# Hybrid attention and delta-rule layer on one core: the planner's date for the first products of the triangular inverse moves from 0.3 to 1.5

## The chip, the cores and the metric

The kernel runs on one core of a Trainium2 chip. The metric is device time in microseconds (us) of one execution, as the median of a few executions. A trace of one execution gives busy times of the engines: PE is TensorE (matmuls; PEld is its weight loads), DVE is VectorE, ACT is ScalarE, POOL is GpSimd, and SP is SyncE, which here only issues transfers.

## What is computed

One layer over 512 tokens of width 1024: a norm, one wide input projection, an attention branch, a delta-rule branch (8 heads, forward and backward, in chunks of 64 tokens), gates, output projections and two more norms. The part that the change touches is the inverse of a unit triangular matrix in each chunk of the delta rule:

```python
decay = jnp.exp(jnp.where(tril, g[..., :, None] - g[..., None, :], -jnp.inf))
L = jnp.tril(jnp.einsum('bhncd,bhnjd->bhncj', k_beta, k) * decay, -1)
T = lax.linalg.triangular_solve(eye + L, jnp.broadcast_to(eye, L.shape),
                                left_side=True, lower=True, unit_diagonal=True)
u = jnp.einsum('bhncj,bhnjv->bhncv', T, v_beta)
w = jnp.einsum('bhncj,bhnjd->bhncd', T, k_beta * jnp.exp(g)[..., None])
```

Behind it a scan over the chunks carries a state per head and direction; its output is normed, gated and projected together with the attention branch.

## The kernel before

**Matrix products in three passes.** A float32 weight slab of 128x1024 is loaded (`wraw`), ACT rounds it to `whi` (a CAST), and DVE or POOL subtracts to get the rest, `wlo`. A product is then lo·hi + hi·lo + hi·hi over 8 pieces of the contraction: lines 534, 535 and 536 in `gemm_t` (a "gemm step" below is one such group of three matmuls of 128x512), and 553 to 555 or 571 to 573 in `gemm_n` and `gemm_k`. This is most of TensorE's work, and it does not depend on the delta rule: slab follows slab in the order that the string `ORDER` gives.

**The delta rule beside it.** The 8 heads go in two groups, g = 0 and g = 1, each with two directions d. For each group `phase_a` makes the triangular blocks (lines 1013 and 1018 on PE, products on DVE), inverts the 32x32 diagonal blocks by 30 dependent steps on DVE (lines 1049 and 1051, tiles `blk`), sends the result through DRAM (`dW`) and gets it back in two tiles `c2`. From these, four copies on ACT write the diagonals of `LT[0]`, four transposes on DVE write `VT[0]`, four copies on ACT write `VT[1]` (the tile of the name `blk` in the trace, line 1084), and four transposes on DVE write the diagonals of `LT[1]`. Then PE merges 32-blocks into 64-blocks, in 64 products at line 1094 (`m1`) and, after a copy of `m1` to SBUF by ACT (line 1100, a tile `c2`), 64 products at line 1107 (`v1`); each is recorded as two small matmuls, so 128 in the trace. Lines 1127 and 1142 merge 64-blocks into 128-blocks in the same way. `phase_b` then scans the chunks: lines 1177 and 1188 multiply with the state, DVE subtracts (line 1181), line 1197 applies the inverse, line 1215 makes the state's increment, line 1221 updates the state on DVE, line 1229 makes the output.

**What sets the order.** Each engine runs its own list of instructions in the order in which they were issued, and that order is fixed when the program is built. A planner, the class `Flow`, decides it with a clock of its own. Every part (a gemm stream, a phase, the tail of a slab) is a generator. `yield "at", t` asks to go on when the planner's clock has reached t, `yield "get", tag` asks for a free buffer, `yield "pe", d` says that PE is taken for d us. Of the parts that are ready, the one with the smallest priority number goes first, so `phase_a` (priority 1) goes before the gemm stream (priority 10) as soon as its date is reached; until then the gemm stream fills PE, if its next slab is due in the planner's clock. Work on the other engines is booked into the first gap of that engine's plan that is long enough, with a fixed estimate of its duration:

```python
def slot(self, engs, dur, dep):
    t = max(self.now + 0.2, dep + 0.15)
    while True:
        at = [self.fit(e, dur, t) for e in engs]
        if all(a == t for a, _ in at):
            return t, [i for _, i in at]
        t = max(a for a, _ in at)
```

So a date in one part moves not only that part. All that is booked after it sees another clock, another set of gaps and other free buffers. `either` (line 237) takes whichever of two engines would finish first in the plan, so an operation can change its engine as well. The dates decide only the order; on the chip an instruction waits for its inputs by semaphores, whatever the plan thought.

The wait at line 1087 stands behind the copies and transposes of lines 1076 to 1085, whose planned ends are `t0`, `t1` and `ready`, and ahead of the products of line 1094.

Of the kernel before, what the change touches and what calls it, by code (L numbers as in the profile page):

```python
# [35 lines left out]
class Flow:  # L36
# [70 lines left out]
    def free(self, tag, t=None):  # L107
        self.slots[tag].append(self.now if t is None else t)
# [75 lines left out]
def layer(ctx, tc, x, xT, pw0, wp1, wt, wba, wn, rows, qkn, hd16, npost, pnorm, dnorm, cs, out):  # L184
# [12 lines left out]
    def A(dur, dep, fn, *a, **k):  # L197
        return op("ACT", dur, dep, fn, *a, **k)

    def V(dur, dep, fn, *a, **k):  # L200
        return op("DVE", dur, dep, fn, *a, **k)
# [793 lines left out]
    def phase_a(g):  # L995
# [11 lines left out]
        ready = 0.0  # L1007
        for c in range(NT):
# [16 lines left out]
            ready = max(ready, tm)  # L1025
# [50 lines left out]
        for q in range(4):  # L1076
            r, lc = r32(q), r32(q % 2)
            t0 = A(0.53, tx[0], act.copy, LT[0][r, :, r], cx[0][r])
            t1 = V(0.6, max(tx[0], tv[0]), dve.transpose, VT[0][r, :, lc], cx[0][r])
        ready = max(t0, t1)  # L1080
        free("c2", ready)
        for q in range(4):
            r, lc = r32(q), r32(q % 2)
            t0 = A(0.53, max(tx[1], tv[1]), act.copy, VT[1][r, :, lc], cx[1][r])
            t1 = V(0.6, tx[1], dve.transpose, LT[1][r, :, r], cx[1][r])
        free("c2", max(t0, t1))
        yield "at", max(t0, t1, ready) + 0.3

        combos = [(0, 0, 1), (0, 2, 3), (1, 1, 0), (1, 3, 2)]
        yield "get", "aux"  # L1090
# [154 lines left out]
    def chain(g):  # L1245
        ae = spawn(phase_a(g), 1)
        yield "ev", ae
        yield "get", f"u{(15, 14)[g]}"
        oo[g] = unit((15, 14)[g], [128, 4, 4, 128])
        yield "get", "blk"  # L1250
        st8 = tile("blk", [128, 2, 4, 128])
        evs = [spawn(phase_b(g, d, ae, st8[:, d]), 1) for d in range(2)]
        for e in evs:
            yield "ev", e
        free("blk")
        for u in (((4, 7)[g], (5, 8)[g], (6, 9)[g], 10, 11, 12, LTu[g, 0], LTu[g, 1])):
            free(f"u{u}")
# [732 lines left out]
```

## Time and profile before

| | us |
|---|---|
| median of three executions | 754.38 |
| lowest, highest | 754.05, 755.21 |
| the profiled execution: time | 755.96 |
| the profiled execution: span from first to last instruction | 754.2 |
| line 1094, first and last start, both groups | 194.6 to 373.5 |
| line 1107, first and last start, both groups | 203.2 to 377.5 |

The profile names a group of instructions by its source line, engine, output tile and input tiles. Many instructions are issued in one helper and carry line 122 (or 102 and 97), so tiles tell them apart. A time in brackets behind a row is the idle time of that engine just before, and what ended it. Matmuls are pipelined: one of 128x512 is shown with 0.39 us, but the next begins about 0.23 us after it, so the distance of two starts is what a matmul costs.

### The profile page before, as it was taken

The numbers are of one execution on the slowest core, as the hardware profiler recorded it, in microseconds if no ns is written. First come the engines' busy times: TensorE is split into PE (matmuls) and PEld (weight loads), VectorE is DVE, ScalarE is ACT, GpSimd is POOL, SyncE is SP. The second block draws the span as 40 slices with busy tenths as digits, with TensorE's granted clock in tenths as the row PEclk, the third lists the DMA queues.
The fourth block names the chain that finished last, engine by engine and source line by source line (L and its number), as shares of the span: only waits on it lengthen the run. The fifth ranks groups of instructions, "written<-read, shape, count | busy, mean of one in ns | idle before, by whom it ended". The sixth has DMA issues, their size and how long they took to land.

```text
span 754.2 us, 11916 instructions
## 1 busy us (share of the span) xinstructions
PE 738.5 (98%) x4441; PEld 618.3 (82%) x4441; DVE 475.3 (63%) x924; ACT 353.2 (47%) x668; POOL 315.6 (42%) x284
## 2 busy tenths in 40 slices
PE   9999999999799999999999999999999999999996
PEld 7687888887688988888789988888888888888885
DVE  4688989977776657998284644538667754313434
ACT  6659484443552346452633136334566633342422
POOL 5836585203223256300531146647446434661501
PEclk9999999999899999999999999999999999999999
DMA  9864556667412144655521134436233446552313
GB/s 348 295 188 128 166 170 191 212 231 237 121 41 70 57 138 142 199 192 188 147 76 54 43 113 139 140 105 215 85 99 112 139 157 209 180 181 98 98 64 118
DMA packets 65993, 110.99 MB, mean 147 GB/s; under 512 B 22352, under 2 KB 31504, under 8 KB 65936
## 3 DMA queue, kind: packets, MB, share of 16 engines
q1 hardware_dynamic: 65648, 109.98, 45.5%
q8 instruction: 35, 0.57, 0.3%
q10 hardware_dynamic: 288, 0.26, 0.1%
q14 instruction: 22, 0.18, 0.1%
HBM read 87.11 MB, written 23.10 MB: 146 GB/s over the span
## 4 chain that ended last, share of the span: by engine, by line
PE 85%; DVE 4%; DMA 4%; ACT 3%; issue 1%; POOL 1%; SPq 0%; POOLq 0%; DVEq 0%; ACTq 0%
PE mm L534 14%; PE mm L535 14%; PE mm L536 14%; PE mm L555 4%; PE mm L553 4%; PE mm L554 4%; PE mm L571 3%; PE mm L572 3%; PE mm L573 3%; PE aux L1197 2%; PE aux L1229 2%; DMA u<-CI 2%; PE mm L1552 2%; DVE f L122 2%; PE aux L1215 2%; PE aux L1188 1%
## 5 line engine op out<-in xcount | busy, mean ns | idle before, releaser
L102 POOL TENSOR_TENSOR wlo<-wraw,whi 128x1024 fp32r<-128x1024 f32 x52 | 124.3, 2394 | 210.2 <-ACT whi L122 169.7
L534 PE MATMUL mm<-u,wlo 128*128 128x512 f32 x504 | 204.3, 405 | 3.3 <-POOL wlo L102 2.8
L536 PE MATMUL mm<-u,whi 128*128 128x512 f32 x504 | 197.4, 392 | 0.0
L535 PE MATMUL mm<-u,whi 128*128 128x512 f32 x504 | 197.2, 391 | 0.0
L534 PEld LDWEIGHTS mm<-u,wlo 128*128 128x128 f32 x504 | 95.2, 189 | 23.2 <-POOL wlo L102 3.3
L536 PEld LDWEIGHTS mm<-u,whi 128*128 128x128 f32 x504 | 94.9, 188 | 20.5
L535 PEld LDWEIGHTS mm<-u,whi 128*128 128x128 f32 x504 | 95.3, 189 | 17.3 <-DVE u L122 0.3
L122 ACT CAST whi<-wraw 128x1024 fp32r<-128x1024 f32 x63 | 65.9, 1048 | 71.1 <-PE mm L536 40.8
L122 DVE SCALAR_TENSOR_TENSOR f<-mm,cw,f 128x510 f32<-128x510 f32 (+1 forms) x96 | 71.6, 746 | 13.7 <-ACT f L122 11.1
L102 POOL TENSOR_TENSOR u<-wraw,u 128x1024 fp32r<-128x1024 f32 x23 | 55.1, 2398 | 13.5 <-ACT u L122 12.8
L122 DVE TENSOR_TENSOR u<-aux,u 128x512 f32<-128x512 f32 (+2 forms) x60 | 39.4, 670 | 20.7 <-ACT u L122 16.7
L553 PE MATMUL mm<-u,u 128*128 128x512 f32 (+1 forms) x136 | 52.0, 382 | 0.0
L555 PE MATMUL mm<-u,u 128*128 128x512 f32 (+1 forms) x136 | 51.4, 378 | 0.0
L554 PE MATMUL mm<-u,u 128*128 128x512 f32 (+1 forms) x136 | 51.3, 377 | 0.0
L122 ACT CAST u<-aux 128x512 fp32r<-128x512 f32 (+1 forms) x28 | 15.6, 556 | 38.8 <-PE aux L1725 13.7
L122 ACT COPY c<-aux 128x512 f32<-128x512 f32 x18 | 10.6, 587 | 47.7 <-DVE f L122 28.7
L122 ACT ACTIVATE mm<-f 128x512 f32<-128x512 f32 x24 | 14.4, 601 | 38.2 <-DVE f L122 32.5
L571 PE MATMUL mm<-whi,u 128*128 128x512 f32 x80 | 31.6, 395 | 0.0
L572 PE MATMUL mm<-wlo,u 128*128 128x512 f32 x80 | 31.3, 391 | 0.0
L573 PE MATMUL mm<-whi,u 128*128 128x512 f32 x80 | 31.2, 390 | 0.0
L102 POOL TENSOR_SCALAR_AFFINE_SELECT u<-u 128x512 f32<-128x512 f32 x16 | 10.1, 640 | 49.8 <-DMA u<-CI 37.5
L555 PEld LDWEIGHTS mm<-u,u 128*128 128x128 f32 x136 | 25.6, 188 | 4.8
(261 smaller groups left out, 1471.6 us busy)
## 6 DMA issues: line engine op xcount, KB each, us to landing
wraw<-in_wt_dram SPq DMA_DIRECT2D x59, 512.0 KB, 3.5
wraw<-in_wn_dram SPq DMA_DIRECT2D x28, 512.0 KB, 4.0
u<-in_wt_dram SPq DMA_DIRECT2D x13, 512.0 KB, 5.7
u<-CI SPq DMA_DIRECT2D x16, 256.0 KB, 5.0
u<-in_x_dram SPq DMA_DIRECT2D x4, 512.0 KB, 6.9
u<-in_xT_dram SPq DMA_DIRECT2D x4, 512.0 KB, 8.2
eD<-u SPq DMA_DIRECT2D x8, 256.0 KB, 7.7
Bdk<-f SPq DMA_DIRECT2D x8, 256.0 KB, 2.8
```

What stands on the lines that cost most here:

```text
L102: ins = fn(*a, **k)
L122: fn(*a, **k)
L534: pe.matmul(o, lo[:, k, :], mh(k), start=(k == 0), stop=False)
L535: pe.matmul(o, hi[:, k, :], ml(k), start=False, stop=False)
L536: pe.matmul(o, hi[:, k, :], mh(k), start=False, stop=(k == 7))
L553: pe.matmul(o, b, hi, start=(i == 0), stop=False)
L554: pe.matmul(o, a, lo, start=False, stop=False)
L555: pe.matmul(o, a, hi, start=False, stop=(i == 7))
L571: pe.matmul(o[t], b, hi, start=(k == 0), stop=False)
L572: pe.matmul(o[t], a, lo, start=False, stop=False)
L573: pe.matmul(o[t], a, hi, start=False, stop=(k == 7))
L1197: pe.matmul(pw[:, h, :], Vm[g][d][:, 4 * c + h, :], r[:, h, :], start=True, stop=True)
```

## The change

One number: the date on which `phase_a` goes on from the copies and transposes to the products of line 1094 is 1.5 behind their planned end instead of 0.3. `phase_a` runs once for each group, so it acts twice.

```diff
@@ -1084,7 +1084,7 @@
             t0 = A(0.53, max(tx[1], tv[1]), act.copy, VT[1][r, :, lc], cx[1][r])
             t1 = V(0.6, tx[1], dve.transpose, LT[1][r, :, r], cx[1][r])
         free("c2", max(t0, t1))
-        yield "at", max(t0, t1, ready) + 0.3
+        yield "at", max(t0, t1, ready) + 1.5
 
         combos = [(0, 0, 1), (0, 2, 3), (1, 1, 0), (1, 3, 2)]
         yield "get", "aux"
```

No instruction is added or removed on PE. What moves is the order, and the order on all engines is the same in both kernels up to the first products of group 0, and again from the middle of group 1's scan (about 403 us in the trace of before) to the end. The numbers behind a tile's name count what was issued before and differ between the two kernels for the same tile. Three places matter.

**Place 1, group 0, PE.** Rows of PE around lines 1094 and 1107, first before, with the end of one slab's product (`mm_1915`), the products of line 1094, the first steps of the next slab (`mm_2041`), and line 1107:

```order
L536 MATMUL mm_1915<-u_15_132,whi_1868 128x512
L1094 MATMUL aux_1968<-blk_1881,u_69_512 32x32 x2
...
L534 MATMUL mm_2041<-u_14_131,wlo_1913 128x512
L535 MATMUL mm_2041<-u_16_133,whi_1912 128x512
L536 MATMUL mm_2041<-u_14_131,whi_1912 128x512
L534 MATMUL mm_2041<-u_14_131,wlo_1913 128x512
L535 MATMUL mm_2041<-u_16_133,whi_1912 128x512
L536 MATMUL mm_2041<-u_14_131,whi_1912 128x512
L1107 MATMUL aux_2051<-u_69_512,c_243_2036 32x32 x2
```

And the same place of PE's list in the changed kernel:

```order
L536 MATMUL mm_1915<-u_15_132,whi_1868 128x512
L1094 MATMUL aux_1970<-blk_1881,u_69_512 32x32 x2
...
L534 MATMUL mm_2040<-u_14_131,wlo_1913 128x512
L535 MATMUL mm_2040<-u_16_133,whi_1912 128x512
L536 MATMUL mm_2040<-u_14_131,whi_1912 128x512
L534 MATMUL mm_2040<-u_14_131,wlo_1913 128x512
L535 MATMUL mm_2040<-u_16_133,whi_1912 128x512
L536 MATMUL mm_2040<-u_14_131,whi_1912 128x512
L534 MATMUL mm_2040<-u_14_131,wlo_1913 128x512
L535 MATMUL mm_2040<-u_16_133,whi_1912 128x512
L536 MATMUL mm_2040<-u_14_131,whi_1912 128x512
L1107 MATMUL aux_2064<-u_69_512,c_243_2038 32x32 x2
```

The products of line 1094 still follow the same slab directly, and the next slab still comes behind them; only line 1107 has moved, by one gemm step.

On ACT the same place reads before (`blk_1882` is `VT[1]`, `c_243` is the copy of `m1`, `f_235` a convolution whose taps run on DVE):

```order
L122 COPY blk_1882<-c_232_1884 32x16x32 x4
L122 CAST whi_1912<-wraw_1760 128x1024
L122 ACTIVATE f_235_1914<-mm_1871,cw 128x512
L122 CAST whi_1962<-wraw_1852 128x1024
L122 ACTIVATE go_1964<-mm_1915 128x512
L122 COPY c_243_2036<-aux_1968 128x512
L122 ACTIVATE mm_1871<-f_235_1914 128x512
```

And in the changed kernel, ACT at the same place:

```order
L122 COPY blk_1882<-c_232_1884 32x16x32 x4
L122 CAST whi_1912<-wraw_1760 128x1024
L122 ACTIVATE f_235_1914<-mm_1871,cw 128x512
L122 CAST whi_1962<-wraw_1852 128x1024
L122 ACTIVATE go_1964<-mm_1915 128x512
L122 ACTIVATE mm_1871<-f_235_1914 128x512
L122 COPY c_243_2038<-aux_1970 128x512
```

The copy of `m1` now stands behind an ACTIVATE that reads what the convolution's taps on DVE have written.

**Place 2, group 1, PE.** Before, around line 1094 of the second group, where a product in the form of lines 571 to 573 (`kv`) runs beside it:

```order
L573 MATMUL mm_3502<-u_368_2887,u_15_132 128x512
L1094 MATMUL aux_3652<-blk_3575,u_209_1688 32x32 x2
...
L571 MATMUL mm_3499<-u_368_2887,u_17_134 128x512
L572 MATMUL mm_3499<-u_368_2887,u_15_132 128x512
L573 MATMUL mm_3499<-u_368_2887,u_15_132 128x512
L571 MATMUL mm_3500<-u_368_2887,u_17_134 128x512
L572 MATMUL mm_3500<-u_368_2887,u_15_132 128x512
L573 MATMUL mm_3500<-u_368_2887,u_15_132 128x512
L1107 MATMUL aux_3728<-u_209_1688,c_471_3717 32x32 x2
```

PE's list at this place in the changed kernel:

```order
L573 MATMUL mm_3497<-u_366_2871,u_15_132 128x512
L571 MATMUL mm_3494<-u_366_2871,u_17_134 128x512
L572 MATMUL mm_3494<-u_366_2871,u_15_132 128x512
L573 MATMUL mm_3494<-u_366_2871,u_15_132 128x512
L571 MATMUL mm_3495<-u_366_2871,u_17_134 128x512
L572 MATMUL mm_3495<-u_366_2871,u_15_132 128x512
L573 MATMUL mm_3495<-u_366_2871,u_15_132 128x512
L1094 MATMUL aux_3658<-blk_3575,u_209_1688 32x32 x2
...
L571 MATMUL mm_3496<-u_366_2871,u_17_134 128x512
```

Here line 1094 has moved behind two groups of three matmuls, and line 1107 with it (two such groups still stand between them).

**Place 3, group 0's scan, DVE.** Before, the first steps of `phase_b` on DVE (`f_265` and `f_268` are the scaled values of the two directions, `c_274` is the subtraction of line 1181 for the first, `f_278` the taps of a convolution):

```order
L122 TENSOR_TENSOR f_265_2288<-aux_2281,dj 128x512
L122 TENSOR_TENSOR f_268_2297<-aux_2290,dj 128x512
L1181 SCALAR_TENSOR_TENSOR c_274_2327<-aux_2322,nec,u_99_845 128x128 x4
L122 SCALAR_TENSOR_TENSOR f_278_2339<-mm_2158,cw,f_278_2339 128x510
L122 SCALAR_TENSOR_TENSOR f_278_2339<-mm_2158,cw,f_278_2339 128x511 x2
L122 SCALAR_TENSOR_TENSOR f_278_2339<-mm_2158,cw,f_278_2339 128x510
L122 TENSOR_TENSOR f_281_2351<-aux_2345,dj 128x512
L122 SCALAR_TENSOR_TENSOR u_115_946<-mm_2158,f_278_2339 128x512
```

And DVE in the changed kernel, from the same two multiplications on:

```order
L122 TENSOR_TENSOR f_265_2292<-aux_2285,dj 128x512
L122 TENSOR_TENSOR f_268_2301<-aux_2294,dj 128x512
L122 SCALAR_TENSOR_TENSOR f_272_2305<-mm_2162,cw,f_272_2305 128x510
L122 SCALAR_TENSOR_TENSOR f_272_2305<-mm_2162,cw,f_272_2305 128x511 x2
L122 SCALAR_TENSOR_TENSOR f_272_2305<-mm_2162,cw,f_272_2305 128x510
L122 SCALAR_TENSOR_TENSOR u_115_946<-mm_2162,f_272_2305 128x512
L1181 SCALAR_TENSOR_TENSOR c_278_2340<-aux_2334,nec,u_99_845 128x128 x4
```

The whole convolution, its four taps and its closing operation, now stands ahead of the first subtraction of line 1181. On PE the product of line 1197 that reads this subtraction stood one gemm step behind lines 1177 and 1188; it now stands three gemm steps, one product of line 1229 and one of line 1177 behind them. Elsewhere in the scan some gemm steps and products change places in the same manner, two copies `u<-c` (128x4x128, the keys of two heads) go from POOL to ACT, and of group 1's chain of 30 steps the convolutions that stand among its first and last steps stand ahead of it or a few steps earlier.

## The prediction

> **What bounds the kernel now.** I read the page's head first, for which engine has no room.
>
> ```profile
> span 754.2 us, 11916 instructions
> PE 738.5 (98%) x4441; PEld 618.3 (82%) x4441; DVE 475.3 (63%) x924; ACT 353.2 (47%) x668; POOL 315.6 (42%) x284
> ```
>
> TensorE is busy for 98% of the span and its instructions stay the same, so an order can only win back what PE loses now, or add to it. Where it loses is in the busy time by stretches of the span (columns: length; busy time and count of PE, PEld, DVE, ACT, POOL; granted clock; DMA).
>
> ```profile
> 194.00:206.00 12.00, 7.98 (x269) 6.08 (x268) 9.17 (x15) 7.48 (x12) 4.69 (x2) 0.72 0.32 102
> 206.00:370.00 164.00, 163.68 (x1018) 140.61 (x1017) 117.83 (x243) 71.98 (x135) 53.26 (x37) 1.00 0.44 135
> 370.00:378.00 8.00, 7.00 (x275) 5.56 (x274) 2.61 (x5) 5.52 (x10) 4.68 (x2) 1.00 0.23 82
> 378.00:747.00 369.00, 368.80 (x1990) 309.08 (x1988) 190.70 (x400) 153.74 (x281) 159.27 (x139) 1.00 0.37 120
> ```
>
> Of what the change can reach, PE idles 4.0 us around group 0's first products (and has 0.72 of its clock there), 1.0 us around group 1's, and 0.32 us in the 164 us between. The two short stretches are the two places of line 1094. The waits of PE say what they are (total, times, longest).
>
> ```profile
> PE mm L534 <- POOL wlo L102: 2.8, 2, 2.3
> PE aux L1094 <- ACT blk L122: 1.8, 2, 1.0
> PE aux L1107 <- issue: 1.0, 1, 1.0
> ```
>
> **Group 0: does the wait go?** The timeline of PE at the first place (start, length, instruction):
>
> ```profile
> 194.65 0.25 PE L1094 MATMUL aux<-blk,u 32*32 32x32 f32 x4
> 195.69 0.22 PE L1094 MATMUL aux<-blk,u 32*32 32x32 f32 x2 [0.80 <-ACT blk L122]
> 196.87 1.24 PE L1094 MATMUL aux<-blk,u 32*32 32x32 f32 x122 [0.95 <-ACT blk L122]
> 200.37 0.79 PE L534 MATMUL mm<-u,wlo 128*128 128x512 f32 x1 [2.26 <-POOL wlo L102]
> 200.96 0.63 PE L535 MATMUL mm<-u,whi 128*128 128x512 f32 x1
> 202.66 0.63 PE L536 MATMUL mm<-u,whi 128*128 128x512 f32 x1
> 203.22 1.93 PE L1107 MATMUL aux<-u,c 32*32 32x32 f32 x128
> 205.09 0.64 PE L534 MATMUL mm<-u,wlo 128*128 128x512 f32 x1
> 205.56 0.40 PE L535 MATMUL mm<-u,whi 128*128 128x512 f32 x1
> ```
>
> PE comes to line 1094 at 194.65, waits 0.80 + 0.95 = 1.75 us for ACT's copies, and is then stopped for 2.26 us by the next slab. ACT and POOL at the same time:
>
> ```profile
> 194.31 2.51 ACT L122 COPY blk<-c 32x512 f32<-32x512 f32 x4
> 196.84 1.04 ACT L122 CAST whi<-wraw 128x1024 fp32r<-128x1024 f32 x1
> 199.79 0.58 ACT L122 COPY c<-aux 128x512 f32<-128x512 f32 x1
> 201.70 0.60 ACT L122 ACTIVATE mm<-f 128x512 f32<-128x512 f32 x1 [1.32 <-DVE f L122]
> ```
>
> ```profile
> 197.96 4.69 POOL L102 TENSOR_TENSOR wlo<-wraw,whi 128x1024 fp32r<-128x1024 f32 x2 [8.71 <-ACT whi L122]
> ```
>
> The copies end at 194.31 + 2.51 = 196.82. Behind them ACT rounds the next slab, and POOL makes its `wlo`, the first of two in 4.69 us: 197.96 + 2.34 = 200.30, where PE goes on. So both waits have one cause, the late copies, and PE has nothing else that is ready. The changed order shows the same here: line 1094 still follows the same slab, the CAST still stands behind the copies, and all ahead of it is unchanged. **The 1.75 us and the 2.26 us stay.** Had line 1094 gone behind a gemm step, PE would have waited until 200.30 for that step instead.
>
> What moves is line 1107, by one gemm step. The stretches behind the waits show what that meets:
>
> ```profile
> 198.00:200.30 2.30, 0.10 (x12) 0.00 (x0) 1.73 (x3) 2.30 (x4) 2.30 (x2) 0.63 0.02 7
> 203.00:205.20 2.20, 2.20 (x130) 1.92 (x129) 0.62 (x2) 0.00 (x0) 0.00 (x0) 0.50 0.70 262
> 205.20:208.00 2.80, 2.80 (x12) 2.35 (x13) 2.68 (x4) 0.00 (x0) 0.00 (x0) 0.96 0.72 232
> ```
>
> The clock falls to half: 0.63 in 2.30 us means half for 2 x 0.37 x 2.30 = 1.7 us, so from 198.6; 0.96 in 2.80 us means half for 0.22 us more, so until 205.4. In this time a large matmul takes (202.66 - 200.96)/4 = 0.425 us instead of 0.227 (by line 534 to 536 elsewhere: 0.68 us for three). Changed, line 1107 begins 3 x 0.425 = 1.28 us later, at 204.50. Its 128 matmuls take 205.09 - 203.22 = 1.87 us at half clock and 0.74 + 0.76 = 1.50 us at full clock (group 1's rows, below). By 205.42 it has done 0.92/1.87 = 49% and needs 51% of 1.50 = 0.76 us more, so it ends at 206.18. Before, PE had done the same work (line 1107 and three large matmuls) at 205.56 + 2 x 0.227 = 206.02. **Term: +0.2 us.** The copy of `m1`, now behind the tanh that begins at 201.70, ends at about 202.9; line 1107 comes at 204.50, so it covers 1.6 us. Without that cover each us would count in full.
>
> By the Trainium skill, page "TensorE: Matmul & The Clock Gate", section "Part 1: The HAM clock gate (the "warmup" mystery)", activity is judged in free-running windows of 3413 ns; the trace agrees, since 198.6 to 205.4 is two of them. By that rule the slow stretch would depend on where the windows happen to lie in an execution.
>
> **Group 1: two groups of three matmuls change places with line 1094.** PE, ACT and DVE there:
>
> ```profile
> 372.47 1.29 PE L1094 MATMUL aux<-blk,u 32*32 32x32 f32 x128
> 375.27 0.74 PE L1107 MATMUL aux<-u,c 32*32 32x32 f32 x63
> 377.01 0.76 PE L1107 MATMUL aux<-u,c 32*32 32x32 f32 x65 [1.00 <-issue]
> ```
>
> ```profile
> 369.14 2.52 ACT L122 COPY blk<-c 32x512 f32<-32x512 f32 x4
> ```
>
> The copies end at 371.66 and line 1094 began 0.8 us later: no wait to remove. It begins now at 372.47 + 6 x 0.227 = 373.83, with 2.2 us of cover; the six matmuls are done ahead of it instead of behind. Sum 0. The 1.00 us inside line 1107 ended with no release ("issue"). The trace has this once in the four runs of 128 small matmuls of lines 1094 and 1107, so I bound it by 0 and 1.0 us for the changed order and take 1.0, as the same runs stand there with six large matmuls between. That group 1's chain on DVE is mixed otherwise with convolutions could spend the cover of 2.2 us; nothing is added to DVE ahead of the chain's end, so I count 0.
>
> **Group 0's scan.** The subtraction of line 1181 now stands behind a whole convolution. I price the place by before's rows (ACT, then DVE, then PE):
>
> ```profile
> 220.65 0.59 ACT L122 COPY c<-aux 128x512 f32<-128x512 f32 x1 [0.31 <-PE aux L1197]
> 224.58 1.05 ACT L122 CAST whi<-wraw 128x1024 fp32r<-128x1024 f32 x1
> 225.53 0.69 ACT L122 ACTIVATE f<-mm,cw 128x512 f32<-128x512 f32 x1
> 229.45 0.60 ACT L122 ACTIVATE mm<-f 128x512 f32<-128x512 f32 x1 [0.50 <-DVE f L122]
> ```
>
> ```profile
> 225.05 1.13 DVE L1181 SCALAR_TENSOR_TENSOR c<-aux,nec,u 128x128 f32<-128x128 f32 x4 [3.09 <-PE aux L1177]
> 226.25 3.10 DVE L122 SCALAR_TENSOR_TENSOR f<-mm,cw,f 128x510 f32<-128x510 f32 x4
> 230.08 0.69 DVE L122 SCALAR_TENSOR_TENSOR u<-mm,f 128x512 f32<-128x512 f32 x1
> ```
>
> ```profile
> 224.79 1.06 PE L1188 MATMUL aux<-blk,u 128*128 128x128 f32 x8
> 225.60 0.47 PE L534 MATMUL mm<-u,wlo 128*128 128x512 f32 x1
> ```
>
> In before's clock the copy on ACT ends at 221.24. In the new list there follow the CAST (to 222.3), the convolution's start (223.0), the taps on DVE (226.1), the tanh (226.7), the closing operation (227.4) and line 1181 (228.5). PE leaves line 1188 at 225.60, does three gemm steps (2.04 us, to 227.65), then lines 1229 and 1177 (0.9 us each, as 224.79 to 225.60 shows about), and asks for the subtraction at 229.4: **0.9 us of cover, no wait.** Both sides start 0.9 us later, by the term above and the step that now stands ahead. PE idles only 0.32 us in the whole stretch, so up to 0.3 us can be won, and a wait of some tenths for a PSUM bank can come: 0.
>
> The two copies that go to ACT (about 0.59 us each, by the copy above) fall where ACT, busy for 72 of 164 us, has gaps. They cost nothing, or 0.6 us once if PE waits for the operation behind.
>
> **Sum:** +0.2 us. Against the profiled execution, 755.96 us (a span of 754.2 and 1.8 around it), that is 756.2; the median is 1.6 us below that execution, so 754.38 + 0.2 = 754.6 us.
>
> **The rivals.**
> - **The taps bind (slower).** If the convolution ahead of line 1181 starts late, because its CAST waits for a transfer or a free buffer, the scan stands. It decides from 0.9 us of delay on; a delay of one run of taps, 3.10 us, costs 3.10 - 0.9 = 2.2 us: 756.8. For it speaks that ACT's list puts the CAST 3 us earlier than before; against it, DVE waits 3.09 us there in before, so there is room.
> - **The stop in line 1107 goes.** Another split of the small matmuls spares the 1.00 us: 753.6. For it: it came once in four. Against: the same neighbours.
> - **The clock does not fall.** If the idle time of group 0 falls across windows differently, about 6 x 0.2 + 0.37 + 0.24 = 1.8 us come back: 752.8. Against it: the idle time is the same, and nothing in the change moves it. (The page above gives the windows.)
> - **The change does what it says**, and the 1.75 us go: 752.8. Against it: the order, and the slab that is ready only at 200.30.
>
> **How the numbers follow.** Forecast, within 1 us of 754.6: 0.65. The stop gone, or tenths won: 0.10. The taps or another new wait: 0.16. Clock or wait gone: 0.09. A measurement of this kernel tells about 0.2% (1.5 us) from no change, so the first two are "within" (0.75), the third slower, the last faster. The range runs from 753.2, below the stop's 753.6, to 756.8, the taps' price.
>
> **What would show it.** Line 1094 of group 0 still waits about 1.75 us for ACT, and line 534 behind it about 2.3 us for POOL; line 1107 of group 0 starts near 204.5; line 1094 of group 1 near 374 without a wait; line 1197 in the scan without one. I am wrong if PE idles more than 0.3 us at one place between 206 and 370, or if the stretch 194 to 206 idles less than 3.5 us.

## The result and the profile after

The changed kernel takes 757.23 us (median of seven executions, 755.09 to 757.99), the kernel before 754.38 (seven, 753.20 to 755.21). The ratio is 1.0030, with an interval from 1.0018 to 1.0043: it is slower by 0.3%, where less than 0.2% either way was forecast as likeliest. The profiled execution after is 757.20 us long.

The page's head after, with the same instructions on PE:

```profile
span 755.5 us, 11910 instructions
PE 740.2 (98%) x4441; PEld 617.9 (82%) x4441; DVE 476.5 (63%) x924; ACT 353.8 (47%) x670; POOL 314.6 (42%) x282
```

The waits of PE after, in the view that groups them (total, times, longest):

```profile
PE mm L534 <- POOL wlo L102: 2.7, 2, 1.8
PE aux L1094 <- ACT blk L122: 1.8, 2, 1.0
PE aux L1107 <- issue: 0.6, 1, 0.6
```

They are the three of before, the first two at about their old sizes and the third smaller. So the totals don't show what was lost; one has to go along the kernel. PE's timeline at group 0's products (the columns as before):

```profile
195.21 0.25 PE L1094 MATMUL aux<-blk,u 32*32 32x32 f32 x4
196.34 0.22 PE L1094 MATMUL aux<-blk,u 32*32 32x32 f32 x2 [0.88 <-ACT blk L122]
197.51 1.69 PE L1094 MATMUL aux<-blk,u 32*32 32x32 f32 x122 [0.96 <-ACT blk L122]
201.02 0.79 PE L534 MATMUL mm<-u,wlo 128*128 128x512 f32 x1 [1.81 <-POOL wlo L102]
204.98 1.29 PE L1107 MATMUL aux<-u,c 32*32 32x32 f32 x128
```

PE comes 0.56 us later than before to this place, over an order that is the same up to here, waits 0.88 + 0.96 = 1.84 us for ACT and is stopped for 1.81 by POOL. Line 1094 itself takes 1.69 instead of 1.24 us in between, because most of its products fall into the half-clock stretch here (from 197.9 us by the clock records, before from 198.6); with the wait behind it that is 3.50 us in both. The waits that the date stands beside are all still there.

To find the rest I compared the starts of the same large matmuls. All kernels of this study run the same 2,680 matmuls with 256 columns or more in nearly one order, so the lag of, say, the 921st behind that of a reference tells what the way there cost. What each kernel loses against one profile of the kernel before (`c0_before`, below) in three stretches, worked out from the starts in the traces, us:

```
                 scan of group 0   to group 1's blocks   inverse of group 1
                 821st to 921st    921st to 1081st       1281st to 1381st
                 (230 to 275 us)   (275 to 321 us)       (367 to 411 us)
before              0.01              0.01                  0.56
after               0.28              0.40                  0.87
c1_after            0.32              1.10                  0.57
g0_only             0.31              1.42                  0.47
g1_only            -0.01              0.00                  0.98
after_swap          0.31             -0.06                  0.58
g0_swap             0.31             -0.07                  0.56
before_swap         0.01              0.91                 -0.12
before_all4         0.05              0.00                  0.08
```

The names are those of the experiments; the first two columns speak clearly, the third has a scatter of its own that the experiments explain.

### The profile page after: what moved, and what is told of

Same layout as the page of the kernel before. It is cut to its first block, busy times and chain, and to the rows that moved or that the text cites. A ratio compares the mean times of both kernels' runs of the same rounds, so it can differ in the third digit from the quotient of the medians.

```text
span 755.5 us, 11910 instructions
## 1 busy us (share of the span) xinstructions
PE 740.2 (98%) x4441; PEld 617.9 (82%) x4441; DVE 476.5 (63%) x924; ACT 353.8 (47%) x670; POOL 314.6 (42%) x282
## 4 chain that ended last, share of the span: by engine, by line
PE 88%; DVE 3%; ACT 3%; DMA 3%; POOL 2%; issue 1%; SPq 0%; POOLq 0%; DVEq 0%; ACTq 0%
PE mm L534 16%; PE mm L535 15%; PE mm L536 15%; PE mm L555 4%; PE mm L553 4%; PE mm L554 4%; PE mm L571 3%; PE mm L572 3%; PE mm L573 3%; PE aux L1229 2%; PE mm L1552 2%; PE aux L1197 2%; PE aux L1215 2%; PE aux L1188 1%; PE aux L1177 1%
```

## The experiments

**The change again, and its two halves.** Line 1087 acts once for each group, so it can be split:

```diff
-        yield "at", max(t0, t1, ready) + 1.5
+        yield "at", max(t0, t1, ready) + (1.5 if g == 0 else 0.3)
```

for `g0_only`, with `g == 1` for `g1_only`; `c0_before` and `c1_after` are the two kernels unchanged.

> The kernel before against itself, to know what a comparison of equals gives. All theories: ratio 1.000, medians within 0.7 us. What it adds: whether a single execution of this kernel spreads by more than 1.5 us, since its profiled execution (755.96 us) stood 1.6 us above its median (754.38). If the half-clock stretch of 6.8 us behind group 0's wait comes and goes between executions, the granted clocks of the runs will differ by about 0.0045 (half of 6.8 in 754) and the times by about 1.8 us.

> The changed kernel again. Theory A (new order of group 0's scan, where the two profiles differ by about 0.25 us) and theory B (group 1's place, where they differ by about 0.35 us): +0.6 us in the sum, 0.1% slower. Theory C (the first comparison's +2.3 us, ratio 1.003, is real and not in the two profiles): again 1.002 to 1.004. Theory D (chance of that comparison, or of the clock's windows): anything from -1 to +1.5 us, ratio within 0.999 to 1.002.

> The date 1.5 for group 0 alone. Every engine's order is that of the changed kernel up to group 1's products and that of before from there. Theory A (the cost is in group 0's scan): all of the changed kernel's loss, +2 us or more if the first comparison holds, else about +0.3 us. Theory B (the cost is at group 1): within 0.5 us of before.

> The date 1.5 for group 1 alone: order of before up to group 1's products, order of the changed kernel from there. Theory A: within 0.5 us of before. Theory B: all of the loss. If the two places add, this and the run for group 0 alone sum to the changed kernel's loss within 0.7 us.

Measured, as ratios to the kernel before: `c0_before` 1.0002 [0.9994, 1.0011], `c1_after` 1.0035 [1.0022, 1.0047], `g0_only` 1.0018 [1.0008, 1.0029], `g1_only` 1.0011 [1.0000, 1.0021]. The loss is real and not chance, as theory D had it, and it has two parts that about add up to it, one for A and one for B: 0.0018 + 0.0011 = 0.0029. `g0_only` has the changed order up to group 1's products (about 370 us) and that of before from there, so each part lies where its group is.

The clock has a share in these ratios that stays open. Of the 40 runs of the kernel before in this round, the 14 with a granted clock of 0.992 or 0.993 took 755.0 us on the mean, the 21 with at least 0.995 took 754.0. All five runs of `c1_after` are of the first sort, with a mean of 756.7 us, and eight of the twelve of `g0_only`, with 756.1. Beside runs of before with the same clock they lose 1.6 and 1.1 us, so the losses stand but are smaller. No run tells whether the later order brings the lower clock or only met it.

In group 0's part the second column of the table stands out. The profile shows a wait there that the kernel before does not have. PE of `c1_after`:

```profile
295.98 0.40 PE L536 MATMUL mm<-u,whi 128*128 128x512 f32 x1
297.24 0.50 PE L534 MATMUL mm<-u,wlo 128*128 128x512 f32 x1 [0.86 <-POOL wlo L102]
```

From start to start that is 297.24 - 295.98 - 0.23 = 1.03 us lost. The first profile of after has only 0.3 there, which is why its totals hid it. Followed back on POOL, ACT and SP in `c1_after`:

```profile
291.01 0.22 POOL L122 TENSOR_TENSOR kinv<-kinv,so 128x16 f32<-128x16 f32 x1 [2.62 <-DVE so L122]
291.61 2.93 POOL L300 TENSOR_TENSOR kinv<-kinv,pw 128x16 f32<-128x16 f32 x1
```

```profile
285.68 1.28 ACT L988 ACTIVATE u<-u,Nj 128x128 f32<-128x128 f32 x4 [2.90 <-DMA u<-E]
288.35 1.28 ACT L988 ACTIVATE u<-u,Nj 128x128 f32<-128x128 f32 x4 [1.40 <-DMA u<-E]
```

```profile
277.94 0.35 SPq L122 DMA_DIRECT2D wraw<-in_wt_dram  x1
281.69 0.32 SPq L122 DMA_DIRECT2D gate_dz<-go  x1
282.06 1.86 SPq L122 DMA_DIRECT2D u<-E  x4
```

And the queue of SP in `c0_before`:

```profile
274.86 0.33 SPq L122 DMA_DIRECT2D wraw<-in_wt_dram  x1
275.24 1.37 SPq L122 DMA_DIRECT2D u<-E  x3
280.40 0.32 SPq L122 DMA_DIRECT2D gate_dz<-go  x1
280.76 0.43 SPq L122 DMA_DIRECT2D u<-E  x1
```

The subject is a tile of group 1, 90 us after the place of the change: its decay factors were put aside in DRAM (`E1`, line 971) and are loaded back (line 980) once group 0 has left the tile `u`. SP issues one transfer after the other. In before, three of the four loads stand ahead of the store `gate_dz`, in after all four behind it, and this store waits for DVE's gate product (it is issued at 280.40 and 281.69). So three of the loads go out from 282.06 instead of 275.24: 3.1 us of that is there already at the transfer ahead of them (`wraw`, 277.94 instead of 274.86), 3.7 us is the store. The scalings of line 988 wait for the loads, the squares and the sums `so` come behind those, then POOL's power of 2.93 us, and behind it the subtraction for PE's next slab, in `c0_before` and in `c1_after`:

```profile
289.77 2.38 POOL L102 TENSOR_TENSOR wlo<-wraw,whi 128x1024 fp32r<-128x1024 f32 x1
```

```profile
294.80 2.38 POOL L102 TENSOR_TENSOR wlo<-wraw,whi 128x1024 fp32r<-128x1024 f32 x1
```

In `c1_after` it ends at 297.18, and PE wanted it at 295.98 + 0.23 = 296.21.

**The same order but for one row.** `hold` postpones the issue of what was booked last and leaves its place in the plan; only SP's list changes.

```diff
+    def hold(self, by):
+        i = max(range(len(self.later)), key=lambda j: self.later[j][1])
+        self.later[i] = (self.later[i][0] + by, *self.later[i][1:]); heapq.heapify(self.later)
...
         td = Q(2, ta, GATES[kind][n], t)
-        free("go", td)
+        free("go", td); F.hold(1.9 if (kind, n) == ("dz", 1) else 0.0)
```

This is `after_swap` and, on `g0_only`, `g0_swap`: the store goes behind the four loads. `before_all4` does it to the kernel before with 0.9 instead of 1.9, so that its fourth load passes the store too. `before_swap` is the reverse, before's loads put behind the store:

```diff
-                tE[g, d, c] = Q(2, tE[g, d, c], lt[:, 4 * c:4 * c + 4, :], E1[c])
+                tE[g, d, c] = Q(2, tE[g, d, c], lt[:, 4 * c:4 * c + 4, :], E1[c]); F.hold((1.9, 1.5, 1.1, 0.0)[c])
```

> The kernel after, with one row of SyncE's queue moved: the gate_dz store that stands ahead of the four reloads u<-E of group 1's decay tile stands behind them; every other row of every engine is as in the kernel after. Theory S (the queue: the reloads wait behind a store that waits for VectorE, so the scalings, the reduce so, GpSimd's kinv chain and then its subtraction wlo come some 4 to 5 us later, and TensorE's L534 waits for wlo): the reloads are issued before 279 us instead of 282.06, the subtraction ends by 293.5 instead of 297.18, the wait of 0.86 us at L534 is gone, and the time is 0.6 to 1.0 us under the kernel after, a ratio of 1.0020 to 1.0027 to the kernel before, where the kernel after had 1.0035. Rival R (the queue is a bystander; the later scan and its extra pauses make GpSimd late): the wait stays within 0.3 us of 0.86 and the ratio stays at 1.003 to 1.004.

> g0_only (the later place for group 0's products alone) with the same row of SyncE's queue moved behind the four reloads. Theory S: the wait for wlo at about 296 us is gone and only the scan's 0.2 to 0.4 us and group 0's site are left: ratio 1.0004 to 1.0010, where g0_only had 1.0018. Rival R: ratio stays at 1.0015 to 1.0022.

> The kernel before, with three of the four reloads u<-E moved behind the gate_dz store on SyncE's queue, as they stand in the kernel after; nothing else moves. Theory S: the reloads are issued at about 280.8 instead of 275.24, GpSimd's subtraction wlo starts some 3 to 4 us later than 289.77 and ends at 295.5 to 296.5, TensorE waits 0.4 to 1.2 us for it at L534, and the time is that much over the kernel before: ratio 1.0005 to 1.0016, so that the queue's order alone makes part of the loss. Rival R: no wait for wlo at L534 there, ratio 0.9995 to 1.0004.

> The kernel before, with the gate_dz store moved behind all four reloads (it stands behind three of them): the fourth reload is issued at about 276.6 instead of 280.76. Theory S: TensorE waits for nothing of this chain in the kernel before, so nothing is gained at once; the chain ends 2 to 4 us earlier and the time is within 0.3 us of before (ratio 0.9996 to 1.0004), unless the wait ahead of group 1's inverse starts earlier for it, which would show as a lower time. Rival R: the same, within 0.3 us.

Measured: `after_swap` 1.0012 [1.0001, 1.0023] where after had 1.0035; `g0_swap` 1.0001 [0.9992, 1.0010] where `g0_only` had 1.0018; `before_swap` 1.0012 [1.0003, 1.0020]; `before_all4` 1.0000 [0.9990, 1.0010]. SP, POOL and PE in `after_swap` (an execution that runs 1.3 us later than `c1_after` at this place: `wraw` is issued at 279.22 there):

```profile
279.62 2.22 SPq L122 DMA_DIRECT2D u<-E  x4
282.97 0.36 SPq L122 DMA_DIRECT2D gate_dz<-go  x1
```

```profile
294.29 2.38 POOL L102 TENSOR_TENSOR wlo<-wraw,whi 128x1024 fp32r<-128x1024 f32 x1
```

```profile
297.49 0.39 PE L534 MATMUL mm<-u,wlo 128*128 128x512 f32 x1
```

The wait is gone in both kernels, from the second column of the table and from PE's waits. The rival, that the queue only stands by, falls. The subtraction still ends at 296.67 though, not before 293.5 as I had written: it runs 0.5 us ahead of `c1_after`'s in clock time and 1.8 us ahead of it beside PE, which asks at 297.49 here. That is enough, with less room than I thought.

Both ratios fell further than expected (1.0020 to 1.0027 and 1.0004 to 1.0010), though the intervals reach into those ranges. The clock is in this too: only three of the twelve runs of `after_swap` have a granted clock of 0.992 or 0.993, where all of `c1_after` had, and their mean of 756.4 us is on too few runs to be set against 756.7. The traces carry the size better: against the kernels with the store moved, the second column is higher by 0.5 us (`after`) to 1.5 (`g0_only`).

In `before_swap` the price came as expected, 0.91 us in the table, at another place. The loads went out at 281.26, and what PE waits for is this:

```profile
284.90 0.39 PE L536 MATMUL mm<-u,whi 128*128 128x512 f32 x1
286.03 1.13 PE L1018 MATMUL aux<-u,u 128*128 128x128 f32 x8 [0.73 <-DVE u L122]
```

DVE's products of `phase_a` need the scaled tile too, and while they wait, no `aux` bank comes free for line 1018 to write. Which consumer of the late loads meets PE first depends on the order around; that one does was the same in both.

**The pause inside group 1's line 1107.** The third column scatters by up to 0.7 us between kernels whose order is the same there. Most of that is the pause which the prediction bounded by 0 and 1.0 us: it was 0.44 us in `c0_before`, 1.00 in before, 0.58 in after, 0.29 in `c1_after`. In all twelve traces that have it, it stands right behind the 4,801st of PE's recorded instructions (matmuls, weight loads and those of its sequencer), whatever the order has put there. The list of queues on the page of `c1_after` suggests why (packets, MB, share of 16 engines):

```profile
q8 instruction: 35, 0.57, 0.3%
```

35 packets of 16 KB, for 4,441 matmuls, as many weight loads and 66 semaphore instructions of PE, are 256 instructions each. Lines 1094 and 1107 are 256 each, done in about 1.2 us. Two kernels move line 1107 of group 1 away from line 1094, by one gemm step and by two:

```diff
         t = A(0.5, 0.0, act.copy, M, m1)
         free("aux", t)
-        yield "at", t + 0.3
+        yield "at", t + (1.0 if g else 0.3)
```

for `v1_one`, with 1.7 for `v1_two`. Behind line 1127 some steps change places with it, as line 1427 in `v1_one`.

> The kernel before, with group 1's second products (L1107) one gemm step later: nine 128x512 matmuls between L1094 and L1107 instead of six, still 27 ahead of L1127. Theory F (the pause inside group 1's L1107, 0.26 to 0.82 us over its quiet length in ten profiles, is TensorE waiting for its own next instructions: in each trace it ends 1.3 to 1.55 us after a 16 KB packet of the queue called instruction has landed, and the block that it takes is the same one in every order): L1107 starts 0.68 us later after L1094, so the pause shrinks by 0.68 us, to 0 to 0.15; the time is 0.2 to 0.7 us under the kernel before, ratio 0.9990 to 0.9998. Rival B (the pause belongs to L1107 itself, its banks or its copies): it stays at 0.26 to 0.82 and the ratio is 0.9996 to 1.0006. Nothing is said against either by the waits at L1127, which keeps its 27 matmuls of cover.

> The kernel before, with group 1's second products two gemm steps later: twelve 128x512 matmuls between L1094 and L1107, and 24 instead of 27 between L1107 and L1127, the same 24 as in the kernel after. Theory F: no pause in L1107 at all (its quiet length is 1.4 us). Theory D (group 1's later place costs because 24 matmuls are 5.44 us and VectorE's eight copies and transposes behind L1107 need 5.8): L1127 takes 2.3 to 2.4 us instead of 2.01, as in every kernel with the later place, and the L1427 behind L1142 has its 0.23 us wait as well, since the order from L1127 on is that of the kernel after. Sum against the kernel before: 0.3 to 0.6 gained on the mean pause, 0.55 lost; ratio 0.9996 to 1.0004. Rival (the 24 matmuls are no cause): L1127 stays at 2.01.

> v1_one once more, to see whether it is faster than before: its ratio was 0.9992 with an interval from 0.9979 to 1.0004. If the shorter pause in L1107 is what it gains, 0.1 to 0.6 us: ratio 0.9992 to 0.9999. In the trace the pause in L1107 again ends 1.3 to 1.55 us after the landing of the instruction packet (theory F), whatever its length.

> v1_one with the gate_dz store behind all four reloads on SyncE as well. The store's place gained nothing alone (1.0000), so the same ratio as v1_one, 0.9992 to 1.0000, and the same relation of packet and pause.

Measured: `v1_one` 0.9992 [0.9979, 1.0004], `v1_two` 1.0001 [0.9991, 1.0010], `v1_again` 0.9990 [0.9978, 1.0002], `v1_all4` 0.9989 [0.9976, 1.0002]. In us from the first start of group 1's line 1094, with the landing of the instruction packet that was begun behind it, from the traces' records of transfers:

```
                packet lands   line 1107 starts   pause ends   pause shown
c1_after           2.43             2.80             3.78         0.29
c0_before          2.71             2.80             3.98         0.44
g0_only            2.98             3.12             4.46         0.59
before             3.12             2.80             4.54         1.00
v1_one             2.86             3.49             4.37         0.16
v1_all4            2.95             3.49             4.36         0.15
v1_again           2.58             3.49              -           none
v1_two             3.54             4.80              -           none
```

The pause of the ten orders with six large matmuls between is 0.29 to 1.00 us by the profile, not 0.26 to 0.82 as the expectation has it.

The pause ends 1.3 to 1.55 us after the landing in all twelve traces that have one, and it vanishes where line 1107 comes to the block later than that. So PE waits there for its own next instructions; the profile itself names no releaser. Line 1107 of `v1_again` in one piece:

```profile
375.57 1.31 PE L1107 MATMUL aux<-u,c 32*32 32x32 f32 x128
```

The Trainium skill, page "Runtime: NRT & Kernel Launch", section "Instruction fetch mechanics", says that an engine's instructions come in blocks of 16 KiB of 256, which the packets here agree with, and that the cost of crossing from one to the next is mostly hidden; here up to 1.00 us of it shows. Each of the three runs with line 1107 one step later (`v1_again` is the kernel `v1_one` once more) measures about 0.1% under before, two of them a little under what was expected, but each interval holds 1, so neither kernel is shown to beat it. All are below the changed kernel.

**Group 1's later place.** `v1_two` has 24 large matmuls between lines 1107 and 1127, as the kernel after has, where before has 27. Line 1127 on PE, in `c0_before`, then in `c1_after`:

```profile
382.49 2.08 PE L1127 MATMUL aux<-blk,u 64*64 64x64 f32 x64
```

```profile
385.32 2.38 PE L1127 MATMUL aux<-blk,u 64*64 64x64 f32 x64
```

It is 2.08 long in all kernels with 27, and 2.37 to 2.41 in the five with 24, `v1_two` among them (2.01 and 2.29 to 2.34 from start to start). What is late is the last of the eight operations of DVE between the two lines, shown in `c1_after` by the first and the last:

```profile
379.75 0.68 DVE L122 TENSOR_SCALAR u<-aux 32x512 f32<-32x512 f32 x1 [5.84 <-PE aux L1107]
...
384.87 0.70 DVE L122 STREAM_TRANSPOSE blk<-u 32x512 f32<-32x512 f32 x1
```

They take 5.82 us; 27 matmuls give 27 x 0.227 = 6.12 us of cover, 24 only 5.44. DVE ends at 385.57. The profile names no releaser, but in all five the second product of line 1127 starts 0.05 or 0.06 us behind that end, so it waits for it. A second wait, 0.23 us, stands ahead of line 1427 in the same five kernels, where an `aux` bank seems to come free late. No releaser is named there either, but in all five line 1427 starts 0.14 or 0.15 us behind the operation of DVE that reads an `aux` bank; in `g1_only` that is until 390.12:

```profile
389.71 0.41 DVE L122 TENSOR_TENSOR u<-aux,u 128x256 fp32r<-128x256 f32 x1
```

```profile
389.80 0.40 PE L536 MATMUL mm<-u,whi 128*128 128x512 f32 x1
390.27 0.41 PE L1427 MATMUL aux<-ident,f 128*128 128x128 f32 x2
```

On the other side the later place did what the change is about. In three of the ten traces with the early place (`g0_only`, `g0_swap`, `v1_two`) ACT's copies end after line 1094 has begun, and it loses 0.2 to 0.6 us to them; in none of the four with the late place. For `v1_two`:

```profile
370.05 2.52 ACT L122 COPY blk<-c 32x512 f32<-32x512 f32 x4
```

They end at 372.57, and line 1094, begun at 371.93, goes on at 372.62. Three in ten against none in four can be chance. Sum for group 1: 0.30 + 0.23 lost, about 0.1 won on the mean, against 0.0011 of 754, or 0.8 us (0.0 to 1.6), measured.

## Why the prediction was right and wrong

**Right: the date doesn't reach group 0's waits.** Line 1094 stayed behind the same slab; 1.84 us for ACT and 1.81 for POOL were forecast as 1.75 and 2.26, and what POOL takes less, line 1094 takes more.

**Right in place, not to be told in size: line 1107 of group 0.** It began at 204.98, that is 204.42 without the 0.56 us that this execution was late: forecast 204.50. The term was +0.2, and it was mis-sized: the 1.50 us at full clock add two lengths as the profile shows them, each with the end of its last matmul in it. From start to start the 128 products take 1.22 us at full clock (group 1's line 1094), and with that the same sum gives 206.04 against 206.02, or 0.0. From the 765th to the 771st large matmul, which spans the line, the four profiles with the later place and two half-clock windows lie between 0.5 us under and 0.4 over `c0_before`, with a mean of 0.0; the six with the place of before and two windows between 0.2 under and 0.2 over, with a mean of -0.05.

**The clock was a coin, not a constant.** That rival stood at 0.09, together with the wait, since "nothing in the change moves it". It varies between executions, though: the clock records show two half-clock windows at this place in ten of the fourteen traces (6.83 us) and one (3.41 us) in four, of both places (`before_all4`, `g1_only`, `v1_one`, `after_swap`), and those four are 0.84 to 0.90 us shorter from the 761st to the 771st large matmul. It is part of the scatter, and the change is not shown to have a hand in it: one of the five traces with the later place of line 1107 has a single window, and three of the nine with the place of before.

**Right: the taps don't bind.** Line 1181 ended at 228.21 + 1.12 = 229.33 and PE asked for it at 230.50, with the forecast order of steps and somewhat more cover:

```profile
228.21 1.12 DVE L1181 SCALAR_TENSOR_TENSOR c<-aux,nec,u 128x128 f32<-128x128 f32 x4
```

```profile
230.50 1.10 PE L1197 MATMUL aux<-c,u 128*128 128x128 f32 x8
```

The tenths that were allowed for either way came to +0.3 us in every kernel with the changed scan. In `c1_after` they are five short pauses of 0.07 to 0.23 us at lines 1215, 1229 and 1188 between 232 and 236 us, less 0.3 us of the wait ahead of line 1215 at 241 us, which is shorter there. No run separates what causes them.

**Wrong: "PE idles only 0.32 us in the whole stretch, so up to 0.3 us can be won, and a wait of some tenths for a PSUM bank can come: 0."** This step took the idle time of before as the measure of what could be lost. It named what changes on PE, ACT and DVE in the scan and never looked at SP's list behind it, where three loads fell behind a store. That was worth 1.3 us by one pair of ratios (0.0018 to 0.0001) and 1.7 by the other (0.0035 to 0.0012), with the clock's share in them open; in the traces it is 0.5 (the first of after) to 1.5. The text had named the sign by which it would be wrong: more than 0.3 us idle at one place between 206 and 370. `c1_after` shows 0.86. Of the rivals "the taps or another new wait" came true, by its second half, which had no mechanism and no price of its own.

**Wrong: "Sum 0" for group 1.** It counted the cover of line 1094's copies, which was not the short one. The new order also takes one of the nine gemm steps between lines 1107 and 1127, and DVE's eight operations there, 5.8 us, were never set against what is left.

**Half right: "I bound it by 0 and 1.0 us for the changed order and take 1.0, as the same runs stand there with six large matmuls between."** The pause stayed, but its length is that of a fetch and differs between executions, so one profile's 1.00 was no figure to carry over; the ten with six matmuls between show 0.29 to 1.00.

**The whole.** By the traces, 754.38 + 0.5 to 1.5 for the loads + 0.3 for the scan + 0.5 to 0.8 for group 1 gives 755.7 to 757.0, beside 757.23 and 756.53 measured in the two rounds. The first lies above the range that was given, 753.2 to 756.8; the ratio times the median of before, 756.6, lies in it, 2.0 us above the forecast of 754.6. That it does is luck: the upper end was the price of taps that bind, which they do not, while of what did cost time the loads were not seen and the scan and group 1 were put at 0.

## What to carry to other kernels

When a number in a planner moves, read the difference of every engine's list to its end, the transfer queue first: a load that falls behind a store on the same queue inherits all that the store waits for, here 3.7 us, and it was paid 90 us behind the edit. Then, for each wait of another engine, count the filler that stands between cause and use before and after, since a busy share of 98% says nothing about how close the next wait is. Two halves of a change, and one row put back, separate such causes at the price of a few runs, but ratios of a few tenths of a percent need the granted clock of the runs beside them.

## What the runs showed of the hardware

- **PE can outrun its own instructions.** 256 instructions of small products last 1.2 us; at group 1's place the packet with the next 256 takes 0.93 to 1.40 us to come, and it is another 1.3 to 1.55 us until PE goes on. With twelve large matmuls (2.7 us) between two such runs there is no pause, with nine (2.0 us) 0.16 us, 0.15 or none, with six 0.29 to 1.00.
- **The same order takes different times at group 0's inverse.** From the 755th to the 761st large matmul, which spans the waits of line 1094 in an order that all kernels share, the profiles lie between 0.6 us under and 0.8 over `c0_before`: so much do the copies' inputs come earlier or later. With the clock, a single profile is no measure for a change of 1 us; the lag along the kernel is.
- **The half clock comes in pieces of 3.41 us.** One or two of them here, and in `after_swap` one more at 68 us where no other trace has one. The Trainium skill, page "TensorE: Matmul & The Clock Gate", section "Part 1: The HAM clock gate (the "warmup" mystery)", gives windows of 3413 ns; the records agree to the nanosecond, and the number of windows is what differs between executions.
